# Two-layer hybrid decoder trunk on one core: the RWKV chunk recurrence with the chunks' inverses applied to all chunks at once

## The chip, the cores and the metric

The kernel runs on one core of a Trainium2 chip. The metric is device time in microseconds (us) of one execution; the smaller the better. In the profile, PE is TensorE's matmul, PEld its weight load, DVE is VectorE, ACT is ScalarE, POOL is GpSimd and SP is SyncE, which issues most DMAs.

## The reference

The input is 512 tokens of 1024 features in float32. Each of two layers adds half a SwiGLU, then a mixer, then half a SwiGLU again. The first layer's mixer is differential attention beside RWKV-7, the second's is sparse attention beside an mLSTM. The change lies in RWKV-7, whose core is a recurrence over the tokens, for 8 heads of 64 features:

```python
def step(S, inp):
    r_t, w_t, k_t, v_t, kk_t, a_t = inp
    S = (S * w_t[:, :, None, :]
         - jnp.einsum('bhvk,bhk->bhv', S, kk_t)[..., None] * (kk_t * a_t)[:, :, None, :]
         + v_t[..., None] * k_t[:, :, None, :])
    return S, jnp.einsum('bhvk,bhk->bhv', S, r_t)
...
_, y = lax.scan(step, S0, (tm(r_h), tm(decay), tm(k_h), tm(v_h), tm(kk), tm(a_h)))
```

Every token's state depends on the one before. `y` is then normalised per head, given a bonus term and a gate, and goes with the attention's output through `ab_w_out` onto `x`.

## The kernel before, in words

All activations are kept with features on the 128 partitions and the 512 tokens along the free axis. Most matmuls take weights and activations that are split into a high and a low part of type fp32r, and each product is three matmuls (lines 247 to 249; in the SwiGLU partly line 507). I call these the dense matmuls. ScalarE makes the high part of a weight (`whi`, line 275) and VectorE the low part (`wlo`, line 276).

The mixer of the first layer (`mix0`) works through a list of steps written by hand, `ORDER0`: projections, RWKV's preparation (`prep`), inverse (`inv`) and recurrence (`chain`), attention (`din`, `attn`) and output projections (`out`). A scheduler of the language then sets the order on each engine; the steps `inv` and `chain` carry a higher priority (`AHEAD`), so that their instructions come as early as their inputs allow, with instructions of other steps between them. Each engine runs its own queue in order.

RWKV works on four pairs of heads, `hp` 0 to 3; a pair fills the 128 partitions, one head in each half (`HALF`). The 512 tokens are cut into 8 chunks (`NCH`) of 64 (`LC`). Within a chunk the recurrence over tokens becomes a triangular system; `rwkv_inverse` makes the inverse `X` of all chunks of a pair. `AR` holds for each chunk the 64 columns of a and the 64 of r, `BK` the ones of b and k, `Sa` and `Sr` their masked products, and `UV` for each chunk the solved u beside v.

`rwkv_chain` then goes from chunk to chunk. Ahead of the loop it multiplies `Sa` with v for all chunks (line 905) and keeps the result in `BV`. In the loop a chunk takes, in turn: the product of a and the state `S` (line 914), an addition of its `BV` (line 916), the product with `X` (line 920), two copies into `UV` by VectorE and ScalarE (lines 921 and 922), the product of `BT` and `UV` (line 926) and the new state (lines 933 and 934). The output products with `Sr` (line 941) are placed between by the scheduler. All of this is plain f32, of 64 x 64 elements a half.

Two resources matter for the change. The matmul results of `rwkv_chain` go to the stream "pc", which has one PSUM bank (`STREAMS0`, `BANKS`), so each product waits until the one before it has been read. The tile name `BV` is not in the table `BUFS`, so it has one buffer, which several tiles of the pair use in turn.

Of the kernel before, what the change touches and what calls it, by code (L numbers as in the profile page):

```python
# [12 lines left out]
AF = mybir.ActivationFunctionType  # L13
# [3 lines left out]
P = 128  # L17
# [9 lines left out]
LC = 64  # L27
NCH = T // LC
# [26 lines left out]
def _constants():  # L55
# [34 lines left out]
HALF = (slice(0, 64), slice(64, 128))  # L90
# [2 lines left out]
BUFS = {  # L93
    "": {"raw": 3, "wsp": 3, "tmp": 3},
    "ffn": {"xi": NT, "xn": 2, "fr": 2, "g": 2, "u": 2, "hhi": HF, "hlo": HF, "sum": 2, "shi": 2, "slo": 2},
    "m0": {"rkv": 4, "wag": 2, "tr": 4, "pc": 2, "AR": 2, "Sr0": 2, "Sr1": 2, "X": 3, "Y": 2, "w1": 2, "S": 7, "Sq": 2,
           "bonus": 1, "dq": 1, "dk": 1, "sm_m": 4, "sm_e": 2, "smT": 1, "z": 4, "ss": 2, "junk": 1},
    "m1": {"mqk": 4, "og": 4, "pair": 2, "mz": 3, "nqs": 2, "nk": 2, "nkl": 2, "nv": 2, "ce": 2, "cst": 2, "nz": 3, "ethi": 2,
           "etlo": 2, "sm_m": 2, "sm_e": 5, "mvt": 1, "hid": 3, "junk": 2},
# [22 lines left out]
class Trunk:  # L122
# [748 lines left out]
    def rwkv_chain(self, hp, R, low):  # L871
        nc = self.nc
        mm = nc.tensor.matmul
        K0 = self.k0
        wa, gl = low
        AR, BK, Sa, Sr, X, pc = R["AR"], R["BK"], R["Sa"], R["Sr"], R["X"], R["pc"]
        v = R["in"][2]

        BT = self.tile("BT", (P, NCH, P))
        for q in range(2):  # L880
            p = self.psum("pc")
            for c in range(4):
                nc.tensor.transpose(p[:, c * P:(c + 1) * P], BK[:, 4 * q + c, :], self.ident)
            nc.scalar.activation(BT[:, 4 * q:4 * q + 4, :].rearrange("p c x -> p (c x)"), p, AF.Copy)
        UV = self.tile("UV", (P, NCH, P))
        vs = self.tile("BV").rearrange("p (m o t) -> p m o t", o=2, t=LC)
        v4 = v.rearrange("p (m o t) -> p m o t", o=2, t=LC)
        for o_ in range(2):
            nc.scalar.activation(vs[:, :, o_, :], v4[:, :, 1 - o_, :], AF.Copy)
        for w_, src in ((0, v), (1, vs.rearrange("p m o t -> p (m o t)"))):  # L890
            p = self.psum("pc")
            for m in range(4):
                nc.tensor.transpose(p[:, m * P:(m + 1) * P], src[:, m * P:(m + 1) * P], self.ident)
            p4 = p.rearrange("p (m x) -> p m x", x=P)
            UVm = UV.rearrange("p (m o) x -> p m o x", o=2)

            nc.vector.tensor_copy(UVm[64:, :, 1 - w_, :64], p4[64:, :, :64])
            nc.scalar.activation(UVm[:64, :, w_, 64:], p4[:64, :, 64:], AF.Copy)


        p = self.psum("pc")
        for c in range(NCH):
            for j, h in enumerate(HALF):
                kr = HALF[1 - j]
                mm(p[h, c * LC:(c + 1) * LC], Sa[j][kr, c, :], UV[kr, c, 64 * j:64 * j + 64], start=True, stop=True)
        BV = self.tile("BV")
        nc.scalar.activation(BV, p, AF.Copy)
        S, Ss = None, []
        for c in range(NCH):
            w1 = BV[:, c * LC:(c + 1) * LC]  # L910
            if S is not None:
                pw = self.psum("pc")
                for j, h in enumerate(HALF):
                    mm(pw[h, :64], AR[h, c, :LC], S[h, :], start=True, stop=True)
                w2 = self.tile("w1", (P, LC))
                nc.vector.tensor_add(w2, pw[:, :64], w1)
                w1 = w2
            pu = self.psum("pc")
            for j, h in enumerate(HALF):
                mm(pu[h, :64], X[h, c, :], w1[h, :], start=True, stop=True)  # L920
            nc.vector.tensor_copy(UV[:64, c, :64], pu[:64, :64])
            nc.scalar.activation(UV[64:, c, 64:], pu[64:, :64], AF.Copy)
            if c < NCH - 1:
                ps = self.psum("pc")
                for j, h in enumerate(HALF):
                    mm(ps[h, :64], BT[:, c, 64 * j:64 * j + 64], UV[:, c, 64 * j:64 * j + 64], start=True, stop=True)
                S2 = self.tile("S", (P, LC))
                decay = pc[:, c + 1:c + 2]
                if S is None:
                    nc.vector.tensor_scalar(S2, ps[:, :64], decay, None, op0=ALU.mult)  # L930
                else:
                    sd = self.tile("Sq", (P, LC))
                    nc.scalar.activation(sd, S, AF.Copy, scale=decay)
                    nc.vector.scalar_tensor_tensor(S2, ps[:, :64], decay, sd, op0=ALU.mult, op1=ALU.add)
                Ss.append(S2)
                S = S2

        py = self.psum("py")
        for c in range(NCH):
            for j, h in enumerate(HALF):  # L940
                mm(py[h, c * LC:(c + 1) * LC], UV[:, c, 64 * j:64 * j + 64], Sr[j][:, c, :], start=c == 0, stop=False,  # L941
                   skip_group_check=True)
        for c in range(1, NCH):
            for h in HALF:
                mm(py[h, c * LC:(c + 1) * LC], Ss[c - 1][h, :], AR[h, c, LC:], start=False, stop=c == NCH - 1,
                   skip_group_check=True)


        y, q = self.tile("BV"), self.tile("W", (P, NCH, LC)).rearrange("p c x -> p (c x)")
        nc.scalar.activation(y, py, AF.Copy)  # L950
        p = self.psum("pc")
        mm(p, K0["blk"], y, start=True, stop=True)
        nc.vector.scalar_tensor_tensor(y, p, -1.0 / 64, y, op0=ALU.mult, op1=ALU.add)
        nc.scalar.activation(q, y, AF.Square)
        p = self.psum("pc")
        mm(p, K0["blk"], q, start=True, stop=True)
        self.act(q, p, AF.Ln, bias=self.gneps[:, 0:1], scale=1.0 / 64)
        self.act(q, q, AF.Exp, scale=-0.5)
        nc.vector.scalar_tensor_tensor(y, y, self.vec("lnw", hp), q, op0=ALU.mult, op1=ALU.mult)
        nc.vector.scalar_tensor_tensor(y, y, self.vec("lnb", hp), R["bonus"], op0=ALU.add, op1=ALU.add)  # L960
        p = self.psum("pc")
        mm(p, R["wag"][:, 1, :], gl, start=True, stop=True)
        out = self.tile("ob")
        nc.vector.tensor_mul(out, p, y)
        return out
# [513 lines left out]
```

## Time and profile before

| what | value |
|---|---|
| median of 3 runs | 2138.5 us (2133.6 to 2138.84) |
| profiled execution, its own time | 2130.63 us |
| span in its trace | 2128.9 us |
| PE busy | 2099.0 us (99%) |
| DVE busy | 1667.9 us (78%) |
| ACT busy | 1085.5 us (51%) |
| DMA, mean | 90 GB/s |

The span reaches from the first to the last instruction that the profiler recorded; the execution's own time is 1.7 us longer. Busy times are those of one execution, so a share tells how full an engine's queue is over the whole span and not which engine is waited for at one place. The first layer's mixer, in which the change lies, takes about the stretch from 364 to 757 us of the span. Idle time of an engine is given with what ended it.

### The profile page before, as it was taken

Reading aid. Unit: us, or ns where it says so; the run is one execution under the profiler, and the core shown is the slowest. Engines: PE = TensorE matmul, PEld = TensorE weight load, DVE = VectorE, ACT = ScalarE, POOL = GpSimd, SP = SyncE. Lnnn points to the kernel's source line nnn. Section 1 sums busy time; section 2 is a strip of 40 time slices with the busy share of each in tenths; the row PEclk is TensorE's granted clock in tenths of the full one; section 3 lists DMA queues with packets and bytes.
Section 4 is the critical chain, followed back from the end, with each engine's and each line's share of the span. In section 5 each row is a group of like instructions: output and inputs, shape, how many; then the busy total and the mean of one; then the engine's idle time right before and its main releaser. Section 6 shows DMA issues by size and latency. Waiting matters only on the chain.

```text
span 2128.9 us, 35206 instructions
## 1 busy us (share of the span) xinstructions
PE 2099.0 (99%) x14028; PEld 1787.2 (84%) x14028; DVE 1667.9 (78%) x2818; ACT 1085.5 (51%) x1911; POOL 68.3 (3%) x70
## 2 busy tenths in 40 slices
PE   8999999999999999999999999999999999999998
PEld 6999998776667679999989999996777768999997
DVE  7887786777778798888859787876687767887885
ACT  6544445534434465544446454453368846544444
POOL 1000002000000020000010000001000001000000
PEclk9999999999999999999999999999999999999999
DMA  4333333221121133333333333336421022333331
GB/s 145 107 111 101 102 105 122 68 60 45 41 60 31 31 99 104 110 96 101 107 92 97 109 102 109 95 95 165 115 63 39 24 62 85 100 114 95 102 107 70
DMA packets 305333, 190.94 MB, mean 90 GB/s; under 512 B 19958, under 2 KB 300304, under 8 KB 305168
## 3 DMA queue, kind: packets, MB, share of 16 engines
q1 hardware_dynamic: 304048, 187.59, 30.1%
q8 instruction: 110, 1.80, 0.4%
q0 software_dynamic: 1120, 1.11, 0.3%
q14 instruction: 55, 0.45, 0.1%
HBM read 181.32 MB, written 2.10 MB: 86 GB/s over the span
## 4 chain that ended last, share of the span: by engine, by line
PE 92%; DVE 4%; DMA 2%; ACT 1%; issue 1%; POOL 0%; SPq 0%; DVEq 0%; ACTq 0%; POOLq 0%
PE ps L507 33%; PE ps L247 15%; PE ps L248 15%; PE ps L249 15%; PE ps L838 2%; DMA wraw<-in_ffa_up_dram 1%; PE ps L1368 1%; PE ps L820 1%; PE ps L1365 1%; DVE wlo L276 1%; PE ps L1171 1%; PE ps L1218 1%; PE ps L1349 1%; PE ps L1024 1%; PE ps L941 0%
## 5 line engine op out<-in xcount | busy, mean ns | idle before, releaser
L275 ACT ACTIVATE whi<-wraw 128x1024 fp32r<-128x1024 f32 (+2 forms) x369 | 322.7, 877 | 316.8 <-PE ps L248 200.0
L276 DVE TENSOR_TENSOR wlo<-wraw,whi 128x1024 fp32r<-128x1024 f32 (+2 forms) x369 | 370.1, 1004 | 75.3 <-ACT whi L275 71.4
L507 PE MATMUL ps<-xi,shi 128*128 128x256 f32 x1800 | 330.4, 283 | 0.0
L507 PEld LDWEIGHTS ps<-xi,shi 128*128 128x128 f32 x1800 | 280.6, 192 | 0.0
L248 PE MATMUL ps<-hlo,whi 128*128 128x512 f32 (+1 forms) x716 | 277.0, 387 | 0.0
L247 PE MATMUL ps<-hhi,whi 128*128 128x512 f32 (+1 forms) x716 | 276.9, 387 | 0.0
L249 PE MATMUL ps<-hhi,wlo 128*128 128x512 f32 (+1 forms) x716 | 276.3, 386 | 0.0
L507 PE MATMUL ps<-xi,slo 128*128 128x256 f32 x900 | 254.5, 283 | 0.0
L247 PE MATMUL ps<-xhi,whi 128*128 128x512 f32 x600 | 244.8, 409 | 2.8 <-ACT x L347 2.6
L248 PE MATMUL ps<-xlo,whi 128*128 128x512 f32 x600 | 242.8, 405 | 0.4 <-DVE xlo L294 0.4
L249 PE MATMUL ps<-xhi,wlo 128*128 128x512 f32 x600 | 242.6, 404 | 0.0
L490 ACT ACTIVATE shi<-sum 128x1024 fp32r<-128x1024 f32 x150 | 158.5, 1059 | 127.0 <-DVE sum L485 78.0
L491 DVE TENSOR_TENSOR slo<-sum,shi 128x1024 fp32r<-128x1024 f32 x150 | 182.8, 1219 | 30.0 <-ACT shi L490 30.0
L507 PEld LDWEIGHTS ps<-xi,slo 128*128 128x128 f32 x900 | 172.6, 192 | 0.0
L507 PE MATMUL ps<-xlo,whi 128*128 128x256 f32 x600 | 169.7, 283 | 0.0
L507 PE MATMUL ps<-xhi,whi 128*128 128x256 f32 x600 | 169.4, 283 | 0.0
L507 PE MATMUL ps<-xhi,wlo 128*128 128x256 f32 x600 | 169.3, 283 | 0.0
L484 DVE TENSOR_TENSOR sum<-wraw 128x512 f32<-128x512 f32 x150 | 98.8, 686 | 81.6 <-DMA wraw<-in_ffa_up_dram 41.5
L249 PEld LDWEIGHTS ps<-hhi,wlo 128*128 128x128 f32 x716 | 134.5, 188 | 27.1
L247 PEld LDWEIGHTS ps<-hhi,whi 128*128 128x128 f32 x716 | 134.7, 188 | 25.7
L248 PEld LDWEIGHTS ps<-hlo,whi 128*128 128x128 f32 x716 | 134.7, 188 | 25.1
L247 PEld LDWEIGHTS ps<-xhi,whi 128*128 128x128 f32 x600 | 113.1, 188 | 30.1 <-issue 3.8
(420 smaller groups left out, 4182.8 us busy)
## 6 DMA issues: line engine op xcount, KB each, us to landing
wraw<-in_ffa_gate_dram SPq DMA_DIRECT2D x44, 512.0 KB, 3.8
wraw<-in_ffa_up_dram SPq DMA_DIRECT2D x44, 512.0 KB, 3.8
wraw<-in_ffb_gate_dram SPq DMA_DIRECT2D x44, 512.0 KB, 3.8
wraw<-in_ffb_up_dram SPq DMA_DIRECT2D x44, 512.0 KB, 3.9
wraw<-in_ffa_down_dram SPq DMA_DIRECT2D x48, 384.0 KB, 3.2
wraw<-in_ffb_down_dram SPq DMA_DIRECT2D x48, 384.0 KB, 3.1
wraw<-in_ab_w_in_dram SPq DMA_DIRECT2D x26, 512.0 KB, 3.9
wraw<-in_cd_w_in_dram SPq DMA_DIRECT2D x18, 512.0 KB, 3.9
```

The lines of the kernel that those rows point to most:

```text
L247: mm(out, w[0], x[0], start=start, stop=False)
L248: mm(out, w[0], x[1], start=False, stop=False)
L249: mm(out, w[1], x[0], start=False, stop=stop)
L275: nc.scalar.activation(h, raw, AF.Copy)
L276: nc.vector.tensor_sub(l, raw, h.bitcast(F32))
L484: nc.vector.tensor_add(t[:, 0], *first)
L490: nc.scalar.activation(hi, t, AF.Copy)
L491: nc.vector.tensor_sub(lo, t, hi.bitcast(F32))
L507: nc.tensor.matmul(out, a[:, j], b, start=first and i + j == 0, stop=i + j == 5, skip_group_check=True)
L820: mm(p[:, c * P:(c + 1) * P], BK[h, 4 * q + c, :], AR[h, 4 * q + c, :], start=True, stop=True)
L838: mm(p[h, c * LC:(c + 1) * LC], lhs[h, c, :], rhs[h, c, :], start=True, stop=True)
L1024: mm(po[:, :P], et[:, j, :], v[:, j, :], start=j == 0, stop=j == i)
```

## The change

The inverse is applied ahead of the loop, to all chunks at once. A new helper `batch` runs one 64 x 64 matmul per half and chunk, 16 in all, into one PSUM bank and has ScalarE copy the bank out. It is called three times per pair: with the identity to transpose a (`aT`), with `X` and `aT`, whose result replaces a in `AR`, and with `X` and `BV`, whose result is kept as `XV`. In the loop the product of `AR` and `S` then gives the inverse's share directly, and VectorE adds `XV` to it while it writes `UV`, one instruction for each half. The product with `X` (line 920 before), the addition into `w1` and ScalarE's copy of the loop go away; the first chunk takes its `UV` from `XV` by two copies. The tile `w1` is gone.

```diff
--- before.py
+++ after.py
@@ -93,7 +93,7 @@
 BUFS = {
     "": {"raw": 3, "wsp": 3, "tmp": 3},
     "ffn": {"xi": NT, "xn": 2, "fr": 2, "g": 2, "u": 2, "hhi": HF, "hlo": HF, "sum": 2, "shi": 2, "slo": 2},
-    "m0": {"rkv": 4, "wag": 2, "tr": 4, "pc": 2, "AR": 2, "Sr0": 2, "Sr1": 2, "X": 3, "Y": 2, "w1": 2, "S": 7, "Sq": 2,
+    "m0": {"rkv": 4, "wag": 2, "tr": 4, "pc": 2, "AR": 2, "Sr0": 2, "Sr1": 2, "X": 3, "Y": 2, "S": 7, "Sq": 2,
            "bonus": 1, "dq": 1, "dk": 1, "sm_m": 4, "sm_e": 2, "smT": 1, "z": 4, "ss": 2, "junk": 1},
     "m1": {"mqk": 4, "og": 4, "pair": 2, "mz": 3, "nqs": 2, "nk": 2, "nkl": 2, "nv": 2, "ce": 2, "cst": 2, "nz": 3, "ethi": 2,
            "etlo": 2, "sm_m": 2, "sm_e": 5, "mvt": 1, "hid": 3, "junk": 2},
@@ -898,6 +898,17 @@
             nc.scalar.activation(UVm[:64, :, w_, 64:], p4[:64, :, 64:], AF.Copy)
 
 
+        def batch(lhs, rhs, out):
+            p = self.psum("pc")
+            for c in range(NCH):
+                for j, h in enumerate(HALF):
+                    mm(p[h, c * LC:(c + 1) * LC], lhs(h, c), rhs(h, j, c), start=True, stop=True)
+            nc.scalar.activation(out, p.rearrange("p (c x) -> p c x", x=LC) if len(out.shape) == 3 else p, AF.Copy)
+            return out
+        aT = batch(lambda h, c: AR[h, c, :LC], lambda h, j, c: self.ident[h, 64 * j:64 * j + 64], self.tile("BV"))
+        batch(lambda h, c: aT[h, c * LC:(c + 1) * LC], lambda h, j, c: X[h, c, :], AR[:, :, :LC])
+
+
         p = self.psum("pc")
         for c in range(NCH):
             for j, h in enumerate(HALF):
@@ -905,21 +916,19 @@
                 mm(p[h, c * LC:(c + 1) * LC], Sa[j][kr, c, :], UV[kr, c, 64 * j:64 * j + 64], start=True, stop=True)
         BV = self.tile("BV")
         nc.scalar.activation(BV, p, AF.Copy)
+        XV = batch(lambda h, c: X[h, c, :], lambda h, j, c: BV[h, c * LC:(c + 1) * LC], self.tile("BV"))
         S, Ss = None, []
         for c in range(NCH):
-            w1 = BV[:, c * LC:(c + 1) * LC]
-            if S is not None:
-                pw = self.psum("pc")
+            cols = slice(c * LC, (c + 1) * LC)
+            if S is None:
+                nc.vector.tensor_copy(UV[:64, c, :64], XV[:64, cols])
+                nc.scalar.activation(UV[64:, c, 64:], XV[64:, cols], AF.Copy)
+            else:
+                pu = self.psum("pc")
                 for j, h in enumerate(HALF):
-                    mm(pw[h, :64], AR[h, c, :LC], S[h, :], start=True, stop=True)
-                w2 = self.tile("w1", (P, LC))
-                nc.vector.tensor_add(w2, pw[:, :64], w1)
-                w1 = w2
-            pu = self.psum("pc")
-            for j, h in enumerate(HALF):
-                mm(pu[h, :64], X[h, c, :], w1[h, :], start=True, stop=True)
-            nc.vector.tensor_copy(UV[:64, c, :64], pu[:64, :64])
-            nc.scalar.activation(UV[64:, c, 64:], pu[64:, :64], AF.Copy)
+                    mm(pu[h, :64], AR[h, c, :LC], S[h, :], start=True, stop=True)
+                nc.vector.tensor_add(UV[:64, c, :64], pu[:64, :64], XV[:64, cols])
+                nc.vector.tensor_add(UV[64:, c, 64:], pu[64:, :64], XV[64:, cols])
             if c < NCH - 1:
                 ps = self.psum("pc")
                 for j, h in enumerate(HALF):
```

The following rows are taken from the order in which the instructions of the two programs stand; a row is source line, operation, output and inputs, and elements written per partition, with a count. One row of an f32 matmul is one matmul of one half. Line 914 before is line 929 after, 926 is 935, 941 is 950, 905 is 916, and line 905 after is the matmul in `batch`.

The first place is TensorE in the last pair's loop, one chunk. Before, from the product of `AR` and `S` to that of `BT` and `UV`:

```order
L914 MATMUL ps<-S,AR 64x64 x2
L247 MATMUL ps<-whi 128x512
L668 MATMUL ps<-c_main,sm_e 128x128 x2
L920 MATMUL ps<-w_7631,X 64x64 x2
L248 MATMUL ps<-wlo,whi 128x512
L249 MATMUL ps<-whi,wlo 128x512
L247 MATMUL ps<-whi 128x512
L941 MATMUL ps<-Sr_6983,UV 64x64
L248 MATMUL ps<-wlo,whi 128x512
L926 MATMUL ps<-UV,BT 64x64 x2
L941 MATMUL ps<-Sr_6985,UV 64x64
```

In the changed kernel, from the product of `AR` and `S` of a chunk to its products with `Sr`:

```order
L929 MATMUL ps<-S,AR 64x64 x2
L247 MATMUL ps<-whi 128x512
L248 MATMUL ps<-wlo,whi 128x512
L950 MATMUL ps<-Sr_7037,UV 64x64
L249 MATMUL ps<-whi,wlo 128x512
L935 MATMUL ps<-UV,BT 64x64 x2
L950 MATMUL ps<-Sr_7039,UV 64x64
```

The product of `w` and `X` no longer stands between them, and with it one group of small matmuls among the dense ones is gone from each chunk.

The second place is TensorE at the head of the same pair's loop, behind the inverse. Before, from the last product of the inverse (line 866) to the first chunk's products (line 920 in two halves, then 941 and 926):

```order
L866 MATMUL ps<-X,W 32x32 x16
L247 MATMUL ps<-whi 128x512
L248 MATMUL ps<-wlo,whi 128x512
L249 MATMUL ps<-whi,wlo 128x512
L920 MATMUL ps<-BV,X 64x64
L247 MATMUL ps<-whi 128x512
L920 MATMUL ps<-BV,X 64x64
L248 MATMUL ps<-wlo,whi 128x512
L249 MATMUL ps<-whi,wlo 128x512
L247 MATMUL ps<-whi 128x512
L941 MATMUL ps<-Sr_6983,UV 64x64
L926 MATMUL ps<-UV,BT 64x64 x2
```

In the changed kernel the product of `X` and `aT` (whose tile is a `BV`) comes first, cut in two by the wait for the second half of `X` (line 631 transposes for the attention, line 639 too):

```order
L866 MATMUL ps<-X,W 32x32 x16
L247 MATMUL ps<-whi 128x512
L248 MATMUL ps<-wlo,whi 128x512
L639 MATMUL ps<-c_main,on 128x128
L631 MATMUL ps<-c_main,t 128x128 x2
L905 MATMUL ps<-X,BV 64x64
L631 MATMUL ps<-c_main,t 128x128 x2
L905 MATMUL ps<-X,BV 64x64 x15
```

Seven rows of the attention follow, and then the 16 products of `Sa` and `UV`. The last of these, and the product of `X` and `BV` behind it:

```order
L916 MATMUL ps<-UV,Sa_7038 64x64
L1022 MATMUL ps<-dkl,dq 128x128
L249 MATMUL ps<-whi,wlo 128x512
L247 MATMUL ps<-whi 128x512
L248 MATMUL ps<-wlo,whi 128x512
L905 MATMUL ps<-BV,X 64x64 x16
```

The products of `Sa` and `UV` stood ahead of the inverse's end before and now stand behind the product of `X` and `aT`; two further batches and the work between them lie between the inverse and the first chunk.

The third place is ScalarE in the changed kernel at the same point, from the copy of the second half of `X` (line 868) to the first chunk's copy into `UV` (line 925); line 906 is the eviction in `batch`, line 918 that of the product of `Sa` and `UV`, and line 183 is an exponential of the attention's softmax:

```order
L868 ACTIVATE X<-ps 32x8x32
L632 ACTIVATE vtok<-ps 128x512
L906 ACTIVATE AR<-ps 128x8x64
L183 ACTIVATE sm_e,z<-ps,sm_m 128x128
L918 ACTIVATE BV<-ps 128x512
L183 ACTIVATE sm_e,z<-ps,sm_m 128x128
L906 ACTIVATE BV<-ps 128x512
L925 ACTIVATE UV<-BV 64x64
```

Before, no row of ScalarE stood between the two copies: line 922 came directly behind line 868, and the eviction into `BV` (line 907) stood 18 rows ahead of that.

## Rows read from the trace of the kernel before

**Rows 1.** The page: busy us (share) and count by engine; its chain by engine.
```profile
PE 2099.0 (99%) x14028; PEld 1787.2 (84%) x14028; DVE 1667.9 (78%) x2818; ACT 1085.5 (51%) x1911; POOL 68.3 (3%) x70
...
PE 92%; DVE 4%; DMA 2%; ACT 1%; issue 1%; POOL 0%; SPq 0%; DVEq 0%; ACTq 0%; POOLq 0%
```

**Rows 2.** Windows: us, then busy us (instructions) by engine, granted clock, DMA share, GB/s.
```profile
380.00:780.00 400.00, 393.72 (x3333) 277.69 (x3332) 309.66 (x602) 185.43 (x393) 12.07 (x7) 1.00 0.18 52
```

**Rows 3.** Waits of PE, 380 to 780 us: total us, times, longest.
```profile
PE ps L247 <- ACT whi L275: 1.2, 3, 0.6
...
PE ps L941 <- DVE UV L921: 0.3, 1, 0.3
```

**Rows 4.** Groups of PE by shape: busy us, mean ns, idle before.
```profile
L838 PE MATMUL ps<-W,Y 64*64 64x64 f32 x512 | 19.4, 222 | 0.5 <-DVE W L845 0.5
...
L920 PE MATMUL ps<-w,X 64*64 64x64 f32 x112 | 9.3, 243 | 0.0
...
L920 PE MATMUL ps<-BV,X 64*64 64x64 f32 x16 | 2.6, 243 | 0.0
```

**Rows 5.** Timeline of PE: start, us, line, tiles, shape, records; one L920.
```profile
705.73 0.40 PE L247 MATMUL ps<-whi 128*128 128x512 f32 x1
705.97 0.40 PE L248 MATMUL ps<-wlo,whi 128*128 128x512 f32 x1
706.29 0.33 PE L920 MATMUL ps<-w,X 64*64 64x64 f32 x4
706.56 0.50 PE L249 MATMUL ps<-whi,wlo 128*128 128x512 f32 x1
706.89 0.40 PE L247 MATMUL ps<-whi 128*128 128x512 f32 x1
```

**Rows 6.** Timeline of PE around one batch of 16 matmuls.
```profile
443.52 0.40 PE L249 MATMUL ps<-xhi,wlo 128*128 128x512 f32 x1
443.75 0.40 PE L247 MATMUL ps<-xhi,whi 128*128 128x512 f32 x1
444.08 1.15 PE L838 MATMUL ps<-W,Y 64*64 64x64 f32 x32
445.16 0.50 PE L248 MATMUL ps<-xlo,whi 128*128 128x512 f32 x1
445.50 0.40 PE L249 MATMUL ps<-xhi,wlo 128*128 128x512 f32 x1
```

**Rows 7.** Groups of DVE and ACT by shape, 380 to 780 us.
```profile
L921 DVE COPY UV<-ps 64x64 f32<-64x64 f32 x32 | 6.9, 215 | 10.9 <-PE ps L920 10.8
...
L916 DVE TENSOR_TENSOR w<-ps,BV 128x64 f32<-128x64 f32 x28 | 6.3, 224 | 11.9 <-PE ps L914 11.8
...
L922 ACT ACTIVATE UV<-ps 64x64 f32<-64x64 f32 x32 | 7.0, 218 | 37.6 <-DVE UV L921 35.5 <-DVE pr L714 1.8
...
L907 ACT ACTIVATE BV<-ps 128x512 f32<-128x512 f32 x4 | 2.4, 595 | 1.4 <-PE ps L905 1.3
```

**Rows 8.** Timeline: an eviction by ACT behind a batch; a load that waits for ACT.
```profile
675.22 0.55 PE L668 MATMUL ps<-c_main,sm_e 128*128 128x128 f32 x3
675.39 0.60 ACT L907 ACTIVATE BV<-ps 128x512 f32<-128x512 f32 x1 [1.31 <-PE ps L905]
...
450.36 0.38 ACT L862 ACTIVATE W<-ps 32x256 f32<-32x256 f32 x1
...
450.78 0.20 PEld L866 LDWEIGHTS ps<-X,W 32*32 32x32 f32 x8 [0.38 <-ACT W L862]
```

**Rows 9.** Group of ACT, 380 to 780 us: the weight split.
```profile
L275 ACT ACTIVATE whi<-wraw 128x1024 fp32r<-128x1024 f32 x34 | 35.3, 1053 | 51.1 <-PE ps L248 47.2 <-issue 3.8
```

**Rows 10.** Timeline: first matmul of the last output projection.
```profile
743.55 0.50 PE L247 MATMUL ps<-AR,whi 128*128 128x512 f32 x1 [0.38 <-ACT whi L275]
```

## The prediction

> **What bounds the kernel now.** I began with the busy shares and the chain that ended last. TensorE is busy for 2099.0 of 2128.9 us, VectorE for 78%, and 92% of the chain lies on TensorE [rows 1]. So the first question is what the change does to TensorE's queue, not how long the RWKV recurrence takes. Next came the stretch that holds the recurrence: the order of instructions is the same in both kernels up to about 410 us and again from the last output projection on (743 us), so only the part between can change. In 380 to 780 us TensorE is busy for 393.72 of 400 us, at a granted clock of 1.00 (2.4 GHz) [rows 2]. It is idle there for 6.3 us in all. Of the idle time that the view of waits names in that stretch, the recurrence's own steps (lines 914 to 934) account for one wait of 0.3 us, for `UV`; the largest entry is a weight split on ScalarE [rows 3]. The scheduler already puts dense matmuls between the links of the recurrence, so a shorter recurrence has almost nothing to give back directly.
>
> **TensorE: what is removed and what is added.** A plain-f32 matmul leaves two records in the trace: L920 stands in the program 64 times and in the trace 112 + 16 = 128 times [rows 4]. Removed per head pair are 16 matmuls (`X` on `w1`, two halves of 8 chunks); added are three batches of 16 (identity on `AR`, `X` on `aT`, `X` on `BV`). Net that is 32 matmuls per pair, 128 in all, 256 records more.
>
> A record and an interruption of the dense stream have different prices, and two places in the trace separate them. Dense matmuls of 512 columns follow each other at 0.23 us. Around one L920 of four records, two dense matmuls and the L920 take 706.89 - 705.97 = 0.92 us [rows 5]; less 2 x 0.23 that is 0.46 us. Around a batch of 32 records it is 445.50 - 443.75 = 1.75 us [rows 6], less 0.46, so 1.29 us. The 28 further records cost 0.83 us, 0.030 us each, and the interruption itself 0.46 - 4 x 0.030 = 0.34 us. One rule of the Trainium skill speaks to the second number: the page TensorEngine Tiling (Array Packing), section Tiling Modes (Key Properties), says that a change of tiling mode drains TensorE. The 0.34 us agrees with a fixed price of this kind. Read as the whole price, with the small matmuls inside free, the rule would turn the sum into a gain; that is a rival below.
>
> Now the counts. I went through both complete orders and counted the stretches between two dense matmuls that hold at least one plain-f32 matmul: 336 before, 322 after. That is fewer saved than one expects from 36 pieces of L920 against 12 batches, because many L920 stood beside other small matmuls already, and some batches are cut in two by the wait for `X` (second place of the order above). So:
> - records: 256 x 0.030 = +7.7 us
> - interruptions: 14 x 0.34 = -4.8 us
> - TensorE's queue: **+2.9 us**
>
> The busy times by group check the size: a batch is 19.4 / 16 = 1.21 us busy, twelve of them 14.5 us, against 9.3 + 2.6 = 11.9 us for all of L920 [rows 4], so +2.6 us.
>
> **VectorE and ScalarE.** Removed are 28 additions into `w` (0.224 us) and 28 of 32 copies into `UV` (0.215 us); added are 56 additions of 64 x 64 out of PSUM, which I take at the same 0.22 us; VectorE's load stays within 0.5 us. ScalarE loses 28 copies of 0.218 us (6.1 us) and gains 12 evictions of 128 x 512 at the 0.595 us of L907 (7.1 us) [rows 7]. With 309.66 and 185.43 of 400 us busy [rows 2] both have room in sum, and I cost this at nothing; if that cover were gone it is about 1 us on ScalarE.
>
> **The new serial links.** Behind the inverse now stand, in turn, `X` on `aT`, eviction into `AR`, `Sa` on `UV`, eviction into `BV`, `X` on `BV`, eviction into the last `BV` tile. The stream "pc" has one PSUM bank and `BV` one buffer, so the product of `Sa` and `UV`, which before was done and evicted while the inverse still ran, now has to follow the `aT` product. Two matmul-to-matmul links per pair hang on a ScalarE eviction, 8 in all. What such a link needs: after L905 the next matmul starts at 675.22, the eviction runs from 675.39 for 0.60 us, and a weight load that waits for ScalarE comes 0.04 us after its end (0.38 us from 450.36, next load 450.78) [rows 8]. That makes 0.81 us from the next matmul's start. In the order of the changed kernel four dense matmuls stand before the last batch (second place above), three of 512 columns and one of 128, about 0.9 us with the changes of kind. So an idle ScalarE just makes it, and nothing is lost. A ScalarE in the middle of a weight split does not: that takes 1.053 us [rows 9]. In that case TensorE's dense matmuls behind the waiting batch stand still too, because its queue is in order. The bounds are therefore 0 and about 1 us per link. I take 0.1 us, near the lower end, because in the order the evictions stand right behind each other or behind exponentials of the softmax: **+0.8 us**. The upper end, 8 x 1.05 = 8.4 us, is kept for the range.
>
> **What the shorter recurrence gives.** Per later chunk one matmul and one step of VectorE leave the chain; at its head three batches join it. In the last pair there are 36 dense matmuls between its last product and the first of the last output projection, against 20 before. But that projection waits for ScalarE's split of the weights (0.38 us at 743.55), not for `ob` [rows 10]. I take nothing for it; the bound is all the idle time of the stretch, -6.3 us.
>
> **Sum.** +2.9 + 0.8 = +3.7 us on the profiled execution's 2130.63 us, so 2134.3. That execution is 7.9 us under the median of the three runs shown, which spread over 5.2 us. On the median the same sum gives 2138.5 + 3.7 = 2142.2; I say **2142**. A difference under 0.3% (6.4 us) can't be told from no change here.
>
> **Rivals.**
> - *Slower: the serial links stall TensorE.* For it: one bank and one buffer force the order, and ScalarE's splits of 1.05 us can stand in front. Against it: ScalarE is busy under half of the stretch. It decides from (6.4 - 2.9) / 8 = 0.44 us per link; at one split before each link the time is 2138.5 + 2.9 + 8.4 = 2149.8. Chance 0.15.
> - *Faster: only interruptions cost.* If a batch cost what a single L920 costs, 0.46 us, the 14 interruptions fewer would give -6.4 us and 2132. The Trainium skill's rule on the drain (TensorEngine Tiling (Array Packing), Tiling Modes), taken alone, would give this. Against it stands the 1.29 us of a batch [rows 6], measured on the same shape. Chance 0.07.
> - *The idle time goes.* If the recurrence stood behind all idle time of the stretch by ways that the view of waits does not name, 2142.2 - 6.3 = 2136, still within 0.3%. Against it: the named causes are others [rows 3]. Chance 0.10.
> - The forecast, TensorE's own work with links that hold: 0.68.
>
> The forecast and the third rival are both within 0.3%: 0.78. Faster by more: 0.07; slower by more: 0.15. The range goes from 2132, the second rival, to 2149, the links at nearly a whole split each.
>
> **What would show it.** Right: the span of TensorE's busy time in 410 to 745 us grows by 2 to 4 us while its idle time stays near 6 us; three batches of line 905 per pair at about 1.2 us busy; the product of `AR` and `S` at the same 0.46 us between dense matmuls. The link step is wrong if TensorE shows waits for `AR` or `BV` from ScalarE of more than 0.4 us each; the price of a record is wrong if the batches cost under 1 us between dense matmuls. A result under 2132 would mean that the recurrence did hold TensorE back, unseen in the waits.

## The result, and the profile after

The changed kernel took 2149.6 us (median of 4 runs, 2146.45 to 2154.68) beside 2136.5 us of the kernel before in the same session; the ratio is 1.0057 with a 95% interval of 1.0039 to 1.0074. That is some 12 us slower by the ratio (13.2 us between the medians), on the side that the forecast of 2142 us gave 0.15. The profiled execution took 2146.45 us with a span of 2144.7 us.

The page's first lines hardly show it (they answer to [rows 1]): TensorE has 256 records and 7.0 us of busy time more, and the shares stay.

```profile
PE 2106.0 (98%) x14284; PEld 1799.1 (84%) x14284; DVE 1671.1 (78%) x2818; ACT 1085.4 (51%) x1895; POOL 68.5 (3%) x70
...
PE 92%; DVE 4%; ACT 2%; DMA 1%; issue 1%; POOL 0%; SPq 0%; DVEq 0%; ACTq 0%; POOLq 0%
```

To place the loss I cut both spans at the norms ahead of and behind the first layer's mixer (line 321). Ahead of it the changed kernel takes 2.9 us more, behind it 2.3 us more (in both parts the program is the same), and in the mixer 10.6 us more. The windows of the mixer, first of the kernel before (columns as in [rows 2]):

```profile
364.80:769.00 404.20, 397.92 (x3350) 281.20 (x3351) 305.92 (x596) 184.09 (x388) 12.07 (x7) 1.00 0.19 54
```

and of the changed kernel, with the windows of 380 to 780 us (it answers to [rows 2]) and 410 to 745 us:

```profile
367.70:782.50 414.80, 402.09 (x3605) 291.04 (x3606) 309.04 (x596) 184.60 (x372) 12.06 (x7) 0.98 0.18 52
380.00:780.00 400.00, 387.29 (x3543) 279.14 (x3542) 302.76 (x583) 175.40 (x361) 12.06 (x7) 0.98 0.17 49
410.00:745.00 335.00, 325.97 (x3288) 232.55 (x3287) 252.93 (x517) 140.63 (x307) 0.00 (x0) 0.98 0.16 44
```

Two things are new. TensorE's idle time in the mixer (length less busy time) goes from 6.3 to 12.7 us, and the granted clock is no longer 1.00. Narrow windows show where; the columns are the same.

```profile
590.00:592.00 2.00, 0.44 (x16) 0.30 (x11) 1.96 (x4) 0.00 (x0) 0.00 (x0) 1.00 0.00 0
592.00:594.00 2.00, 0.74 (x1) 0.34 (x2) 1.99 (x4) 0.00 (x0) 0.00 (x0) 0.86 0.00 0
594.00:596.00 2.00, 2.00 (x20) 0.93 (x20) 1.99 (x3) 0.00 (x0) 0.00 (x0) 0.50 0.00 0
596.00:598.00 2.00, 2.00 (x27) 1.83 (x25) 0.97 (x2) 0.37 (x1) 0.00 (x0) 0.79 0.19 49
...
698.00:700.00 2.00, 0.69 (x4) 0.42 (x4) 1.96 (x3) 0.45 (x1) 0.00 (x0) 0.81 0.00 0
700.00:702.00 2.00, 1.75 (x35) 1.71 (x36) 1.29 (x4) 0.19 (x1) 0.00 (x0) 0.50 0.00 0
702.00:710.00 8.00, 8.00 (x86) 6.44 (x84) 2.60 (x5) 2.46 (x8) 0.00 (x0) 0.53 0.01 2
```

TensorE runs nearly dry (0.44 of 2 us busy) while VectorE is busy for 1.96 to 1.99 of 2 us, and behind that the clock stands at 0.50, that is 1.2 instead of 2.4 GHz. By the records of the granted clock these half-clock stretches last 3.4 us from 593.4, 10.2 us from 699.2, and 3.4 us from 757.3: 17.0 us, which cost about half their length, 8.5 us (two dense matmuls behind each other start 0.43 us apart there, at 758.22 and 758.65, instead of 0.23). The mixer before has none.

That holds for the profiled execution of the kernel before, whose granted clock over the whole span, 0.999, is as high as any on record for it. Over 23 other executions of it, beside later runs, the clock is 0.995 to 0.998, 0.9967 in the mean; the four of the changed kernel have 0.990 to 0.994. Taken as the span times what the clock lacks to 1.00, an estimate, the clock costs about 7 us before and 17 us after. So it makes up most of the loss over all executions as well.

The waits of TensorE in 380 to 780 us name what was late (they answer to [rows 3]: engine and line that waits, what for, total us, times, longest):

```profile
PE ps L798 <- DVE rkv L796: 2.8, 1, 2.8
PE ps L668 <- DVE sm_e L1029: 2.0, 1, 2.0
PE ps L247 <- ACT AR L579: 1.0, 1, 1.0
...
PE ps L248 <- DVE AR L580: 0.8, 1, 0.8
PE ps L860 <- DVE Y L849: 0.8, 1, 0.8
```

Before, the wait for line 796 was there too, but shorter:

```profile
PE ps L798 <- DVE rkv L796: 1.1, 1, 1.1
```

None of the lines that wait or are waited for in these entries belongs to the recurrence's loop or to the new batches. Line 796 is the bonus term's product in the preparation of the last pair, line 1029 a step of the attention's softmax, and `AR` of lines 579 and 580 the high and low part of the attention's output ahead of the last output projection. The timeline of VectorE (start, us, line, tiles) shows what stood in front of it: the step comes between subtractions for the attention's next inputs (lines 998 and 1005), which TensorE needed only later.

```profile
694.28 0.67 DVE L1005 TENSOR_TENSOR dkl<-t,dk 64x512 fp32r<-64x512 f32 x1
695.22 0.69 DVE L998 TENSOR_TENSOR dq<-t,dq 64x512 fp32r<-64x512 f32 x1 [0.27 <-ACT dq L997]
...
697.19 0.69 DVE L998 TENSOR_TENSOR dq<-t,dq 64x512 fp32r<-64x512 f32 x1
697.91 0.75 DVE L1029 SCALAR_TENSOR_TENSOR sm_e<-sm_e,z 128x512 f32<-128x512 f32 x1
698.69 0.69 DVE L1005 TENSOR_TENSOR dkl<-t,dk 64x512 fp32r<-64x512 f32 x1
```

So the account of the mixer's 10.6 us in these two executions is +6.4 us idle, +8.5 us for the clock, and what is left, about -4.3 us, is TensorE's own work.

### The profile page after: what moved, and what is told of

Its sections match the earlier page's. It is cut to its first block, busy times and chain, and to the rows that moved or that the text cites. A ratio compares the mean times of both kernels' runs of the same rounds, so it can differ in the third digit from the quotient of the medians.

```text
span 2144.7 us, 35719 instructions
## 1 busy us (share of the span) xinstructions
PE 2106.0 (98%) x14284; PEld 1799.1 (84%) x14284; DVE 1671.1 (78%) x2818; ACT 1085.4 (51%) x1895; POOL 68.5 (3%) x70
## 4 chain that ended last, share of the span: by engine, by line
PE 92%; DVE 4%; ACT 2%; DMA 1%; issue 1%; POOL 0%; SPq 0%; DVEq 0%; ACTq 0%; POOLq 0%
PE ps L507 34%; PE ps L247 15%; PE ps L248 15%; PE ps L249 15%; PE ps L838 1%; PE ps L1377 1%; PE ps L1374 1%; PE ps L820 1%; PE ps L905 1%; PE ps L1180 1%; DVE wlo L276 1%; PE ps L1227 1%; PE ps L1033 1%; PE ps L1358 1%; PE ps L1359 0%
```

## The experiments

I set four theories against each other. C: the change makes the scheduler order everything anew, the new order lets TensorE run dry behind VectorE at places outside the recurrence, and the clock falls there. W: the added matmuls cost more than they save. L: the serial links over ScalarE and the one buffer of `BV` hold TensorE (the slower rival of the prediction). O: most orders are bad and the one before was a lucky one.

The table gives each kernel's median, its ratio to the kernel before with the interval, and from its profiled execution the length of the mixer, TensorE's idle time in it, the time at half clock in it, and **work**: TensorE's busy time there less half of the half-clock time, that is, about what the queue would take at full clock with no wait. The sections behind the table explain its names; the subtraction of line 1005 stands in line 996 of the kernel before.

| kernel | median us | ratio [95%] | mixer | idle | half clock | work |
|---|---|---|---|---|---|---|
| before | 2136.5 | 1 | 404.2 | 6.3 | 0 | 397.9 |
| changed | 2149.6 | 1.0057 [1.0039, 1.0074] | 414.8 | 12.7 | 17.0 | 393.6 |
| changed, chain 300 | 2133.2 | 0.9987 [0.9974, 0.9999] | 403.1 | 9.2 | 3.4 | 392.2 |
| before, chain 300 | 2140.2 | 1.0016 [1.0004, 1.0028] | 408.7 | 7.5 | 10.2 | 396.1 |
| changed, own buffer for `aT` | 2160.8 | 1.0114 [1.0094, 1.0134] | 431.4 | 21.6 | 30.7 | 394.4 |
| before, 3 needless batches | 2182.4 | 1.0217 [1.0197, 1.0237] | 452.1 | 21.2 | 44.4 | 408.7 |
| changed, line 1005 on GpSimd | 2131.8 | 0.9980 [0.9969, 0.9991] | 401.7 | 7.0 | 3.4 | 393.0 |
| the same, chain 300 | 2133.8 | 1.0000 [0.9989, 1.0011] | 402.7 | 8.1 | 0 | 394.6 |
| before, line 996 on GpSimd | 2137.7 | 1.0008 [0.9996, 1.0020] | 406.7 | 5.3 | 0 | 401.4 |
| changed, inv 300 | 2139.9 | 1.0013 [1.0001, 1.0026] | 408.9 | 9.7 | 6.8 | 395.8 |
| changed, chain 200 | 2138.2 | 1.0019 [1.0005, 1.0032] | 409.6 | 8.8 | 10.2 | 395.7 |
| before, line 920 twice | 2144.5 | 1.0042 [1.0028, 1.0056] | 411.6 | 9.3 | 6.8 | 398.9 |
| changed, filler at 798 | 2136.4 | 0.9998 [0.9988, 1.0009] | 405.0 | 8.3 | 0 | 396.7 |
| changed, filler and GpSimd | 2148.0 | 1.0061 [1.0045, 1.0076] | 416.2 | 12.8 | 13.6 | 396.6 |

Each ratio is taken against runs of the kernel before on the same chip beside it. The half-clock time differs from one execution to the next, so the last four columns belong to one execution and not to the median.

### The order alone: another priority for the chain, in both kernels

```diff
-AHEAD = {"inv": 200, "chain": 700}
+AHEAD = {"inv": 200, "chain": 300}
```

> The changed kernel with the priority step of the recurrence at 300 instead of 700: the same instructions in another order. Theory C: another order moves the waits for VectorE and the stretches at half clock, so the time moves by several us either way, with the mean clock. Theory W: within 3 us of the changed kernel, 2147 to 2153 us. Theory L: as W, since the links stay.

> The kernel before with the same other priority step of 300, nothing else. Theory C: a control; if order alone moves the time by 5 us or more, with stretches at half clock, the change needs no work of its own to explain 13 us. Theories W and L: 2134 to 2140 us, as the kernel before.

By one number that changes no instruction the changed kernel becomes some 15 us faster (by the ratios), and then stands slightly ahead of the kernel before. The same number costs the kernel before 3 us. C holds: the matmuls and links are all still there. W and L can't explain it. The wait of 2.8 us at line 798 is still there, with a half-clock stretch of 3.4 us from 589.2 behind it; the other two stretches are gone. The view of windows of the changed kernel with 300 shows that one stretch, and full busy time where TensorE ran dry at 698 us:

```profile
588.00:590.00 2.00, 2.00 (x26) 1.24 (x27) 2.00 (x4) 0.96 (x2) 0.00 (x0) 0.81 0.00 0
590.00:592.00 2.00, 2.00 (x19) 1.79 (x17) 1.95 (x3) 1.75 (x4) 0.00 (x0) 0.50 0.03 7
...
698.00:702.00 4.00, 4.00 (x71) 3.13 (x72) 1.23 (x3) 0.80 (x2) 0.00 (x0) 1.00 0.00 0
```

### The buffer that several tiles share

```diff
-        aT = batch(lambda h, c: AR[h, c, :LC], lambda h, j, c: self.ident[h, 64 * j:64 * j + 64], self.tile("BV"))
+        aT = batch(lambda h, c: AR[h, c, :LC], lambda h, j, c: self.ident[h, 64 * j:64 * j + 64], self.temp())
```

> The transposed a gets a buffer of its own, so the product of Sa and UV no longer follows the product of X and aT. Theory L (the new serial links over ScalarE and the one BV buffer cost the time): 2137 to 2141 us, most of the 13 us back. Theory C (the new order makes TensorE wait for VectorE at a few places, the granted clock falls to 1.2 GHz there, and waits and slow stretches are the cost): the time moves only as far as the order of pair 3 changes; stretches at half clock decide, not the waits at line 916. Theory W (the added matmul records cost it): no change, 2147 to 2152 us.

With a buffer of its own for `aT` the kernel is slower still, 2160.8 us, with 30.7 us at half clock. So taking the shared buffer away does not give the time back, and L falls in this part; the order moved with the buffer, and the edit shows again how much that can cost.

### The matmuls alone: three batches in the kernel before

The batches multiply `AR` with the identity, and their results are thrown away; ScalarE copies them out as in `batch`.

```diff
+        for _ in range(3):
+            p = self.psum("pc")
+            for c in range(NCH):
+                for j, h in enumerate(HALF):
+                    mm(p[h, c * LC:(c + 1) * LC], AR[h, c, :LC], self.ident[h, 64 * j:64 * j + 64], start=True, stop=True)
+            nc.scalar.activation(self.temp(), p, AF.Copy)
         p = self.psum("pc")
```

> The kernel before with three batches of 16 matmuls per pair and their evictions added, whose results are thrown away; the loop keeps its three products. Prices of the prediction (1.29 us a batch among dense matmuls): +15.5 us, 2150 to 2154 us, if the order stays harmless. If batches are nearly free: 2137 to 2142 us. Theory C: in addition up to 10 us with a lower mean clock, if the order turns bad.

The time rises by 46 us, far over any price of the matmuls. The window of the mixer says what it is made of:

```profile
364.30:816.40 452.10, 430.90 (x3734) 304.77 (x3735) 308.84 (x596) 190.64 (x400) 12.06 (x7) 0.95 0.17 48
```

Of the 47.9 us by which the mixer grows, 14.9 are idle time and 22.2 the half clock; the work grows by 10.8 us, 0.9 us for each of the 12 batches. That is rough, since the work of the kernel before differs by 5 us between its three orders in the table. The forecast's price, 1.29 us with its interruption and 0.96 us for the records alone, is of the right size, and the records alone are nearer.

### One line off VectorE, in both kernels

Line 1005 is one of the subtractions that stood around the late softmax step. It runs as 8 instructions.

```diff
-            nc.vector.tensor_sub(kl[rows, c, :], t[rows], k[rows, c, :].bitcast(F32))
+            nc.gpsimd.tensor_sub(kl[rows, c, :], t[rows], k[rows, c, :].bitcast(F32))
```

> The changed kernel with the subtraction that makes the low part of the attention's keys on GpSimd instead of VectorE (8 instructions of 0.69 us), the rest as it is; the order shifts behind it. Theory C (TensorE runs dry where VectorE is late, and the granted clock falls there): the wait of 2.0 us for the softmax row at 699 us and the 10 us at half clock behind it go, 2134 to 2142 us. Rival W (work of the change): 2147 to 2152 us. Rival O (any order but a lucky one is bad): anything from 2135 to 2160 us with waits for VectorE elsewhere.

> The same move of the 8 subtractions to GpSimd, with the recurrence's priority step at 300. Theory C: at least as fast as the order at 300 alone, 2126 to 2134 us, with idle time of TensorE in the mixer below 10 us. Rival O: 2130 to 2150 us.

> The control for the variant of the changed kernel with the attention's key subtraction (line 1005) on GpSimd: the same one edit in the kernel before, which keeps its products with X in the loop. Theory C (in the changed kernel TensorE ran dry behind VectorE and the clock fell there, so the edit paid 18 us by mending that): the kernel before had no half-clock stretch in the mixer and about 7 us of idle time there, so the edit can give at most 2 to 3 us, or cost some by another order: 2131 to 2142. Theory P (taking those 64 or so instructions from VectorE pays by itself, whatever the kernel): the same 18 us, 2117 to 2120. Theory W2 (the changed kernel's own work on TensorE is about 3 us less than that of the kernel before): at an order without half-clock stretches this kernel's mixer, less its idle time and half of its half-clock time, comes to 395 to 398 us, against 391 to 394.9 of the kernels with the change.

In the changed kernel the edit gives some 16 us (by the ratios), and the result, 2131.8 us, beats both kernels. Together with chain 300 it gives 2133.8 us, not more than either alone; both mend the same place at 699 us. In the kernel before, where the same subtraction is line 996, it gives nothing (+1.7 us, with an interval from -0.9 to +4.3), so it pays by what it mends in the changed kernel, itself or by the new order that it brings, and not by the load that it takes away. The work of that kernel, 401.4 us, lies over the 395 to 398 that were expected. At the place of the longest stretch the windows of the changed kernel with this edit read:

```profile
692.00:696.00 4.00, 4.00 (x53) 3.40 (x52) 3.74 (x6) 2.92 (x7) 1.34 (x1) 1.00 0.02 4
696.00:700.00 4.00, 4.00 (x44) 2.67 (x42) 1.70 (x3) 2.22 (x5) 1.75 (x2) 1.00 0.42 131
700.00:704.00 4.00, 4.00 (x49) 2.81 (x50) 2.35 (x9) 1.95 (x7) 0.00 (x0) 1.00 0.02 4
```

### Two other orders of the changed kernel

One has "inv" at 300 instead of 200, the other "chain" at 200 instead of 700.

> The changed kernel with the inverse's priority step at 300 instead of 200: the same instructions, another order late in the mixer (from pair 2 on). Theory C: the time follows the idle time of TensorE and the half-clock stretches of this order; span of the mixer less idle time less half of the half-clock time stays at 391 to 394 us. Rival W: the whole mixer stays at 413 to 416 us whatever the order.

> The changed kernel with the recurrence's priority step at 200. Theory C as for the step of 300 of the inverse: 391 to 394 us of the mixer without idle time and without half of the half-clock time; total 2130 to 2150 us. Rival W: 413 to 416 us of mixer.

Both come out 8 to 9 us better (by the ratios) than the changed kernel as it stands, and 3 to 4 us over the kernel before. Their work, 395.8 and 395.7 us, lies somewhat over the 391 to 394 that were expected: it isn't the same in every order. Theory O in its plain form falls: of the changed kernel's orders the five by other priorities or by line 1005 are all within 5 us of the kernel before, and only the one with a buffer for `aT` is clearly worse than the change as it stands. What is left of O is that the kernel before, as it stands, is the fastest of the three orders of it that ran.

### What the removed product costs

Line 920 is taken twice in the kernel before, the second time into a tile that nothing reads.

```diff
             for j, h in enumerate(HALF):
                 mm(pu[h, :64], X[h, c, :], w1[h, :], start=True, stop=True)
+            p2 = self.psum("pi")
+            for j, h in enumerate(HALF):
+                mm(p2[h, :64], X[h, c, :], w1[h, :], start=True, stop=True)
```

> The kernel before with every product of X and w1 (line 920) taken twice, the second into another PSUM tile that nothing reads: 64 extra matmuls, 128 records, thrown away. It prices what the change removes. By the prediction's prices (0.030 us a record, 0.34 us an interruption, and hardly any new interruption because the copy stands beside the original): +3.8 us, 2139 to 2140, mixer less idle and half of half-clock time about 401 us. By the price which the earlier runs suggest (the removed products cost about 2.8 + 12 x 0.98 = 14.5 us, because each of the 32 groups also breaks into the dense stream): between +7 and +15 us if the copies stand apart from the originals in the order, mixer corrected to 404 to 412 us. If the scheduler's order comes out badly, some half-clock stretches on top, which the correction takes out.

The time rises by 9 us (6 to 12), but in the profiled execution the mixer's work only by 1.0 us; 3.0 us are idle time and 3.4 the clock. In the timeline of TensorE the copy (line 924) stands right behind the original:

```profile
709.24 0.40 PE L247 MATMUL ps<-whi 128*128 128x512 f32 x1
709.56 0.33 PE L920 MATMUL ps<-w,X 64*64 64x64 f32 x4
709.73 0.28 PE L924 MATMUL ps<-w,X 64*64 64x64 f32 x4
709.94 0.49 PE L1027 MATMUL ps<-vtok,smT 128*128 128x128 f32 x2
```

Four more records next to others move the following matmul by 0.21 us at most. That is of the size of the forecast's record price (0.12 us for four). It does not tell what the removal of whole groups from the dense stream gives.

### Needless work in a dry place

Four matmuls of 128 x 512 stand ahead of line 798 in the last pair, and what they write is overwritten.

```diff
-        p = self.psum("pi")
+        p = self.psum("pi"); [mm(p, K0["blk"], v, start=True, stop=True) for _ in range(4 if hp == 3 else 0)]
         mm(p, K0["blk"], r, start=True, stop=True)
```

> The changed kernel with four matmuls of 128 x 512 in plain f32 put ahead of line 798 in the last pair, results overwritten: some 3.6 us of needless work where TensorE waited 2.8 us for VectorE and where the clock then stood at half for 3.4 us. The scheduler's order behind it changes too. Theory C: no half-clock stretch within 10 us behind line 798; the needless work costs little there. What the new order does at the other dry places (the attention's exponential at 699 us) is open: 2135 to 2152. Theory W or L (the loss is work or serial links): the added 3.6 us come on top, 2151 to 2156.

The kernel does more and is 13 us faster than the changed kernel. The timeline of TensorE at the place where it had stood for 2.8 us:

```profile
586.34 1.15 PE L838 MATMUL ps<-W,Y 64*64 64x64 f32 x32 [0.37 <-DVE W L845]
587.42 3.70 PE L797 MATMUL ps<-rkv,c_rwkv 128*128 128x512 f32 x8
590.95 1.02 PE L798 MATMUL ps<-rkv,c_rwkv 128*128 128x512 f32 x2
```

Two windows of the same kernel behind that place:

```profile
592.00:594.00 2.00, 2.00 (x38) 1.61 (x38) 2.00 (x4) 0.32 (x1) 0.00 (x0) 1.00 0.00 0
594.00:596.00 2.00, 2.00 (x37) 1.77 (x37) 1.33 (x3) 0.28 (x1) 0.00 (x0) 1.00 0.67 198
```

The clock stays at 1.00 there, and the whole mixer has no half-clock stretch. The edit also moves the order behind it, so the stretches at 699 and 757 us went by the order, and only the one at 593 us can have gone by the filler itself. The product of line 796 was also to be moved to GpSimd together with line 1005; that kernel gave no time, so what its wait costs by itself is not measured.

### Both at once

The filler and line 1005 on GpSimd.

> Both edits that paid in the changed kernel at once: the key subtraction of line 1005 on GpSimd, and the four needless matmuls ahead of line 798. Alone the first gave 2131.8 us with one half-clock stretch of 3.4 us left at 594 us, just behind line 798, and the second 2136.4 us with none in the mixer. Theory C: the stretch at 594 us goes as well; its 1.7 us are about what the needless work costs beyond the wait that it fills (3.6 us against 2.8), so 2130 to 2136, no half-clock stretch in the mixer. If the two gains added in full, as they would if each removed a cost of its own and not the same dry places, it would be 2119 us. Theory W or L: the needless work costs its 3.6 us, 2134 to 2137, with the stretch still there.

My own expectation failed as well as that of full gains: 2148.0 us, no better than the changed kernel. Part of the reason can be read. In the order of this kernel two of VectorE's products meet the subtractions on GpSimd. GpSimd and VectorE in the timeline:

```profile
586.82 1.27 POOL L1005 TENSOR_TENSOR dkl<-t,dk 64x512 fp32r<-64x512 f32 x1 [124.03 <-ACT dk L1004]
588.75 1.27 POOL L1005 TENSOR_TENSOR dkl<-t,dk 64x512 fp32r<-64x512 f32 x1 [0.66 <-POOL dkl L1005]
...
587.13 1.51 DVE L787 TENSOR_TENSOR tr<-tr 128x512 f32<-128x512 f32 x1
589.20 2.08 DVE L789 TENSOR_TENSOR BK<-tr 64x512 f32<-64x512 f32 x2
```

The same two steps took 0.68 and 1.34 us in the kernel with the filler alone. The 0.83 + 0.74 = 1.57 us that they lose come back as TensorE's wait for `W`, which grows from 0.37 to 1.94 us; the filler stands behind that wait in the queue, and its matmuls run into a half-clock stretch of 3.4 us from 593.8. TensorE at that place:

```profile
592.43 1.15 PE L838 MATMUL ps<-W,Y 64*64 64x64 f32 x32 [1.94 <-DVE W L845]
593.50 5.40 PE L797 MATMUL ps<-rkv,c_rwkv 128*128 128x512 f32 x8
```

This explains why the filler gives nothing there, and not the whole loss: with line 1005 on GpSimd alone, the same products are slowed alike (1.51 and 2.07 us), with the same wait of 1.94 us for `W` and a stretch of 3.4 us from 593.9, and that kernel is the fastest in the table. What the kernel with both has beside it comes later: half-clock stretches of 6.8 us from 703.0 and 3.4 us from 761.1, and waits of 2.0 and 2.8 us (for `t` of line 563 and `AR` of line 579). Which part of the order makes them was not tried.

## Why the prediction was wrong

The forecast was no difference that can be told. The time is 0.57% longer, clear of the 0.3% and just over the range's end of 2149.

**The step that failed** is "What the shorter recurrence gives. [...] I take nothing for it; the bound is all the idle time of the stretch, -6.3 us". I bounded what the moved work could give by the idle time that was there, and didn't bound what it could take. Idle time rose by 6.4 us, and the granted clock, which stood at 1.00 in [rows 2] and which I took as given, fell for 17 us of the stretch. The rise comes from places that the change doesn't touch, in their new order. That it is the order is shown by the priorities, which give some 15 us back with the same instructions; that dry places behind VectorE are part of it is shown by line 1005 and by the filler. What in the change brings the attention's subtractions in front of its softmax was not tried by itself.

**TensorE's queue, +2.9 us.** The records were priced well: line 905's batches take about 1.15 us busy at full clock (4.6 us for four, below) against the forecast's 1.2. The sum has the wrong sign. The work in the mixer is 392.2 to 395.8 us in the seven kernels with the change and no filler, and 396.1 to 401.4 in the three orders of the kernel before: means of 394.2 and 398.5, so -4.3 us, with a scatter in each group nearly as large. The mis-sized term is most likely that of the interruptions (-4.8), and by the trace it is their count and not their price. Counted over the mixer's records, the tile shape of TensorE's matmuls (`128*128`, `64*64` and so on in the rows) changes 370 times before and 321 times after. Those are 49 changes fewer, where 14 interruptions, with one change in and one out, make 28: the forecast counted stretches between dense matmuls and not the changes among the small and the attention's matmuls inside them. Within the seven kernels the work goes with that count, from 392.2 us at 307 changes to 395.8 and 395.7 at 326 and 328. A linear fit of the work by changes and records, over the twelve profiled executions without the filler, gives 0.19 us a change and 0.027 us a record, as estimates. So an interruption of two changes is 0.37 us, near the forecast's 0.34, and the sum for the change is -9.1 + 7.0 = -2.1 us. No run changes the count alone, so this is an account and not a proof.

**VectorE and ScalarE, nothing.** The new additions cost what was forecast: lines 930 and 931 take 6.0 and 6.4 us. In sum the mixer's busy time moves by 3.1 us on VectorE, where at most 0.5 was forecast, and by 0.5 on ScalarE. The new instructions of VectorE (13.1 us with the first chunk's copies) and those that they replace (13.2) cancel; where its 3.1 us come from isn't shown. But "room in sum" was the wrong question: VectorE was busy for 1.96 of 2 us where TensorE ran dry.

**The serial links, +0.8 us: right.** Groups of TensorE of the changed kernel in 380 to 780 us by shape (columns as in [rows 4]):

```profile
L905 PE MATMUL ps<-X,BV 64*64 64x64 f32 x128 | 6.8, 246 | 0.0
L916 PE MATMUL ps<-UV,Sa 64*64 64x64 f32 x128 | 4.6, 221 | 0.1
L905 PE MATMUL ps<-BV,X 64*64 64x64 f32 x128 | 4.6, 221 | 0.0
L905 PE MATMUL ps<-c_main,AR 64*64 64x64 f32 x128 | 4.5, 220 | 0.1
```

The waits of its weight loads, over the whole span:

```profile
PEld ps L905 <- ACT BV L918: 1.5, 4, 0.4
...
PEld ps L916 <- ACT AR L906: 0.6, 2, 0.4
```

No matmul of lines 905 or 916 stood for more than 0.1 us, and the loads' waits of 0.4 us at most lie beside other matmuls. (The first group took longer because one batch ran at 1.2 GHz.) So the slower rival named the right side and the wrong mechanism, and the range's upper end of 2149, priced for it, lies near the result by accident.

**The landmarks.** The product of `AR` and `S` held: dense matmuls start at 716.09 and 717.01 us around one, 0.92 us, as around line 920 in [rows 5]. I expected TensorE's busy time in 410 to 745 us to grow by 2 to 4 us with idle time near 6 us; it fell by 5.0 us to 325.97, and idle time in that window rose from 4.1 to 9.0 us. Before:

```profile
410.00:745.00 335.00, 330.93 (x3069) 229.63 (x3067) 257.26 (x529) 146.69 (x335) 0.00 (x0) 1.00 0.15 43
```

And the last output projection, which waited for a weight split in [rows 10], now waits for the attention's output.

**What the change is worth.** With the same edit on both sides the changed kernel is faster both times: 0.9987 / 1.0016 with chain 300 and 0.9980 / 1.0008 with the subtraction on GpSimd, 0.997 each; the two intervals of a quotient, taken together as the root of the sum of squares, leave 0.9954 to 0.9988. That is about 6 us for these two pairs. But the same edit makes another order on each side, and one order is a draw: the kernel before stands at 1 to 1.0016 in its three orders, the changed kernel at 0.9980 to 1.0019 in the five by other priorities or line 1005, with means of 1.0008 and 1.0000. So what the change is worth apart from its order isn't shown. As it was made, with the priorities of before, it loses 12 us.

## What to carry to other kernels

On an engine at 98 to 99%, a structural change can move more time by the order that a scheduler makes of everything else than by its own instructions, as it did here; look in the new order for what VectorE has in front of each thing that TensorE waits for, and give a term for lost cover, with a bound upwards. Judge such a change after tuning the priorities again, over several orders on both sides. Gains from mending an order need not add, since each edit makes a new one.

## What the runs showed of the hardware

In a queue that is otherwise full, waits of 2.8 us (line 798), of 2.0 and 0.8 us (lines 668 and 860) and of 1.0 and 0.8 us (lines 247 and 248) each stood ahead of a fall of the granted clock to 0.50, for 3.4, 10.2 and 3.4 us, so that the clock cost more than the added idle time. It need not fall: before, TensorE waited 1.1 us for the same product of line 796 with no half-clock stretch behind it, and in the changed kernel with line 1005 on GpSimd and chain 300 it waited 1.7 us for it with none. The Trainium skill, TensorE: Matmul & The Clock Gate, section "A second HAM failure mode: psum-queue depth-cycling", tells of another kernel whose frequent short idles between groups of matmuls make the clock swing between its two levels; the trace agrees in so far as 12.7 us of idle time in 414.8 us went with three swings. That frequent idles make them it doesn't show: here one or two waits stood ahead of each fall.

A product of two SBUF tiles on VectorE took 1.51 instead of 0.68 us while GpSimd ran a subtraction of 1.27 us. The Trainium skill, GPSIMD Engine Reference, section 1, says that GpSimd's interface to SBUF is shared with VectorE and that VectorE's instructions with two SBUF inputs contend for it; the trace agrees.
